# Two-layer mixture-of-experts block with a delta-net block behind it: expert weights in tiles of 256 rows, later modulation blocks, entry loads in pairs

## The chip, the core and the metric

The program runs on one core of a Trainium2 chip. The core has a matrix engine (TensorE, PE in the profile; PEld is its weight load), a vector engine (DVE), an activation engine (ACT), GpSimd (POOL), a sync engine (SP) that here issues nearly all transfers, and 16 DMA engines between HBM and the on-chip memory (SBUF, 128 partitions; PSUM for sums of matmuls). The metric is the device time of one execution in microseconds (us); lower is better. All data are fp32.

## What is computed

512 tokens of width 1024, and 256 context tokens, go through two layers, then through a second block (gated delta rule, dilated attention, a gated FFN). Of a layer this matters here:

```python
mods = silu(c) @ ada_w[l] + ada_b[l]          # 6 x 1024 numbers: shift, scale, gate of both halves
h = rms_norm(x, n1) * (1 + sc1) + sh1
p = split(h @ w_in)                           # 2304 columns: a_b a_c a_h b_v b_g c_q c_k c_v d_q d_k d_v
x = x + g1 * (concat(short_conv, conv31, window_attention, global_attention) @ w_out)
h2 = rms_norm(x, n2) * (1 + sc2) + sh2
gates, idx = top_k(softmax(h2 @ router).T, 64)     # 16 experts, each takes 64 tokens (32 of the context)
y = (silu(h2[idx] @ w_gate) * (h2[idx] @ w_up)) @ w_down     # three 1024 x 1024 matrices an expert
x = x + g2 * zeros.at[idx].add(y * gates)
```

Layer 0 does all of it for the context too (with modulations of its own), layer 1 only reads the context as keys and values. An expert's weights are 3 x 4 MB and are used once, so a layer streams 201 MB of them.

## The kernel before

One program, in this order: entry, layer 0 (mixing, w_out, routing, experts), layer 1 (the same), the second block. A tile scheduler puts each engine's instructions in order; an engine then runs its own list strictly in that order and waits at each instruction for the semaphores it needs. SP is such an engine: a transfer that must wait for a free buffer holds up all transfers behind it on SP. SP's transfers go round eight completion semaphores, and one waits until the transfer eight places ahead of it on SP has landed.

*Modulations.* `ada_gen` (L310) makes the 6144 numbers of a layer in 12 blocks of 512 columns. A block is four loads of 512 KB (`ada_load`, L196), matmuls (L318), an eviction (L323), transposes (L327) and two DVE steps. Having issued the matmuls of block b it loads pieces of block b+1 ahead, three or four of them (the `if` before L323). Layer 0's mixing runs blocks 4 to 11 of layer 0 and 0 to 7 of layer 1 beside the dense projections. Blocks 8 to 11 of layer 1 are run in layer 0's routing: one after the logits, the others between the steps of the top-k.

*The small pool.* All loads that are neither expert slots nor entry tiles use one pool of five `raw` tiles of 128 x 1024 (512 KB): modulation pieces, columns of w_in and w_out, and five expert tiles.

*Entry.* Small rows, x, the modulation blocks 0, 2, 1, 3 of layer 0 into a tile of their own (`ada0`), the context, and the first columns of w_in. The two tiles of c_q and of d_q take 64 columns from each of two places (`colload2`, L493; at the entry L272), which is 256 bytes a row. Then `norm1_first` (L390 to L398) makes h, split into a high and a low part (`hh`, `hl`), for all eight k.

*Dense projections.* `dense` (L427) goes over units of 128 columns. A unit's 512 KB are split by ACT (L442, `wh`) and POOL (L443, `wl`), and three products each (hh wh, hl wh, hh wl) over eight k are summed in PSUM (L473 for x, L475 for the context). Attention (L553 to L584) and the 31-tap convolution run between.

*Routing.* Logits (L974), softmax, eight rounds of max, index and replace on DVE (L1146 to L1149) for the top 64. The normalized tokens go to DRAM as `hd` (L1132), and each expert's tokens are gathered from it (L1209), transposed (L1221), and get shift and scale on eviction into `xt` (L1225 for x, L1228 for the context). In layer 0, `sumx` and `sumc` in DRAM are zeroed here (L1138, 3 MB): most experts add their output to them by an indirect transfer (L1300), the last are summed by matmuls with one-hot matrices.

*Experts.* Order of the work: gate of e, down of e-1, up of e. Each is eight tiles of 128 rows (`run_gu`, `down`, with `prod` L1237 in layer 1, L1243 and L1248 in layer 0). `wload` (L1044 to L1055) loads tiles in the order of use, one for each one used, into slots: A (18 or 20, tiles `rawA`), W (the five `raw`), B (2 or 8, `rawB`): 25 tiles in layer 0, 33 in layer 1. silu (L1273) and product (L1281) give `sa`, which is transposed (L1290, L1295) to `hT` for down. At the end of layer 0, `sums_load` brings back sumx and sumc, and `sums_add` (L1317 to L1321) transposes and adds them: the context's in the up of expert 15, x's in its down.

```python
slots = ["A"] * nA + ["W"] * 5 + ["B"] * nB
...
    SY.dma_start(r, W[w][l, e, 128 * u:128 * u + 128, :])
```

## Time and profile before

| | us |
|---|---|
| median of 3 runs (2655.12 to 2670.03) | 2669.66 |
| the profiled execution | 2663.15 |
| its span | 2660.6 |
| PE busy in the span | 2472.6 (93%) |
| mean granted clock of PE | 0.974 |

The profiled execution is 2.55 us longer than its span, and 6.5 us under the median. A stretch of the span is named by its start in us: entry 0 to 75, layer 0's mixing and w_out to 456, its routing to 501, its experts to 1056, layer 1's mixing and w_out to 1361, its routing to 1388, its experts to 1867, and the second block to 2660. "Busy" of PE counts a matmul from start to modelled end, so that a PE that waits a little for each weight tile can still read as busy all the time; there the DMA share (1 is all 16 engines busy) and the bytes tell which of the two sets the pace.

### The profile page before, as it was taken

The page shows a single profiled execution, that of the slowest core. Times are in us where ns is not written, and L with a number is a line of the kernel's source. Part 1 is how long each engine was busy: PE and PEld are TensorE (multiplying, and loading weights), DVE is VectorE, ACT ScalarE, POOL GpSimd, SP SyncE. Part 2 cuts the span into 40 slices and gives each one's busy share as a digit, 9 for nine tenths or more (in the row PEclk, how much of TensorE's full clock was granted, in tenths as well). Part 3 has the DMA queues.
Part 4 walks back from the last instruction along what each step waited for, and adds up shares of the span by engine and source line. Part 5 has one row for each costly group of instructions (what it writes and reads, how often), then busy time and mean ns, then how long its engine had stood idle before and what let it go on. Part 6 is the DMA issues. An engine that isn't in the chain of part 4 may idle for free.

```text
span 2660.6 us, 41308 instructions
## 1 busy us (share of the span) xinstructions
PE 2472.6 (93%) x16415; PEld 1498.3 (56%) x16415; DVE 1091.2 (41%) x2371; ACT 870.0 (33%) x1769; POOL 637.3 (24%) x552
## 2 busy tenths in 40 slices
PE   6999999799999999799979989898899999999998
PEld 3776777344444333677743212132578787888876
DVE  4488853311111114689641201021674555444411
ACT  4534362211111111465532111110552435434322
POOL 3423112011111100633220000000433323444443
PEclk9999999899999999799989999999899999999999
DMA  8455455999999998221279999999321102333321
GB/s 284 136 163 141 148 191 195 320 385 387 387 386 385 388 389 296 61 60 48 84 285 391 394 400 400 399 404 408 108 64 27 38 25 72 95 95 96 98 84 63
DMA packets 324758, 584.08 MB, mean 220 GB/s; under 512 B 36864, under 2 KB 190007, under 8 KB 323927
## 3 DMA queue, kind: packets, MB, share of 16 engines
q1 hardware_dynamic: 311943, 555.16, 57.6%
q0 software_dynamic: 12480, 26.23, 4.1%
q8 instruction: 129, 2.11, 0.3%
q14 instruction: 62, 0.51, 0.1%
q10 hardware_dynamic: 144, 0.08, 0.0%
HBM read 556.74 MB, written 18.87 MB: 216 GB/s over the span
## 4 chain that ended last, share of the span: by engine, by line
PE 65%; DMA 18%; DVE 9%; issue 3%; POOL 2%; ACT 1%; SPq 1%; ACTq 0%; DVEq 0%; POOLq 0%
PE px L473 20%; PE ax L1243 4%; DMA rawA<-in_w_down_dram 4%; PE yx L1243 3%; PE ux L1243 3%; PE g L473 2%; DMA rawA<-in_w_up_dram 2%; PE y L584 2%; PE px L475 2%; DMA rawA<-in_w_gate_dram 2%; PE s L553 2%; PE ux L1237 2%; PE pt L565 2%; PE ac L1248 2%; PE ax L1237 2%
## 5 line engine op out<-in xcount | busy, mean ns | idle before, releaser
L443 POOL TENSOR_TENSOR wl<-raw,wh 128x512 fp32r<-128x512 f32 (+1 forms) x312 | 408.7, 1313 | 968.0 <-ACT wh L442 908.2
L442 ACT ACTIVATE wh<-raw 128x512 fp32r<-128x512 f32 (+1 forms) x312 | 193.7, 625 | 440.5 <-PE px L473 207.7
L473 PE MATMUL px<-hh,wh 128*128 128x512 f32 x768 | 314.2, 410 | 6.4 <-DVE xT L1401 1.8
L473 PE MATMUL px<-hh,wl 128*128 128x512 f32 x768 | 311.8, 406 | 6.5 <-POOL wl L443 6.5
L473 PE MATMUL px<-hl,wh 128*128 128x512 f32 x768 | 313.7, 409 | 4.1 <-DVE hl L1019 1.9
L1225 ACT ACTIVATE xt<-tr,mod,a 128x64 f32<-128x64 f32 x256 | 87.0, 405 | 297.6 <-PE tr L1221 287.3
L473 PEld LDWEIGHTS px<-hh,wh 128*128 128x128 f32 x768 | 147.8, 193 | 40.9 <-issue 6.1
L473 PEld LDWEIGHTS px<-hh,wl 128*128 128x128 f32 x768 | 147.9, 193 | 39.5 <-POOL wl L443 7.2
L473 PEld LDWEIGHTS px<-hl,wh 128*128 128x128 f32 x768 | 148.2, 193 | 37.8 <-issue 3.8
L1369 DVE SCALAR_TENSOR_TENSOR Yx<-yx,gcol,Yx 64x512 fp32r<-64x512 f32 x36 | 27.0, 750 | 266.9 <-ACT Yx L1368 266.9
L1209 POOL DMA_INDIRECT xg<-hd,gidx x32 | 29.7, 928 | 432.2 <-PE tr L1221 399.0
L785 DVE SCALAR_TENSOR_TENSOR yT<-ub,cols,yT 128x512 f32<-128x512 f32 (+1 forms) x180 | 126.3, 717 | 0.6
L1243 PE MATMUL ax<-rawA,xt 128*32 128x512 f32 x856 | 117.2, 596 | 1.9 <-DMA rawA<-in_w_gate_dram 1.9
L1273 ACT ACTIVATE sa<-ax 128x512 f32<-128x512 f32 x32 | 19.1, 597 | 287.8 <-PE ax L1243 182.7
L1300 POOL DMA_INDIRECT sumx<-ys,place x14 | 22.0, 1571 | 376.7 <-ACT ys L1347 376.7
L1243 PE MATMUL ux<-rawA,xt 128*32 128x512 f32 x800 | 106.1, 594 | 0.9 <-DMA rawA<-in_w_up_dram 0.9
L1237 PE MATMUL ux<-rawA,xt 128*64 128x512 f32 x328 | 87.5, 611 | 8.3 <-DMA rawA<-in_w_up_dram 8.2
L1237 PE MATMUL yx<-rawA,hT 128*64 128x512 f32 x316 | 80.7, 610 | 12.6 <-DMA rawA<-in_w_down_dram 11.8
L565 PE MATMUL pt<-tab,P 128*128 128x128 f32 x448 | 83.7, 288 | 7.0 <-DVE PT L571 4.3
L1368 ACT ACTIVATE Yx<-yx,gcol 64x512 fp32r<-64x512 f32 x36 | 24.6, 682 | 191.1 <-PE yx L1237 139.3
L1228 DVE TENSOR_SCALAR xt<-tr,a,mod 128x32 f32<-128x32 f32 x128 | 39.1, 310 | 114.7 <-ACT xt L1225 114.2
L1237 PE MATMUL ax<-rawA,xt 128*64 128x512 f32 x316 | 77.4, 612 | 8.1 <-DMA rawA<-in_w_gate_dram 7.5
(593 smaller groups left out, 4887.5 us busy)
## 6 DMA issues: line engine op xcount, KB each, us to landing
rawA<-in_w_gate_dram SPq DMA_DIRECT2D x186, 512.0 KB
rawA<-in_w_up_dram SPq DMA_DIRECT2D x182, 512.0 KB
rawA<-in_w_down_dram SPq DMA_DIRECT2D x151, 512.0 KB
raw<-in_ada_w_dram SPq DMA_DIRECT2D x80, 512.0 KB
raw<-in_w_down_dram SPq DMA_DIRECT2D x74, 512.0 KB
raw<-in_w_gate_dram SPq DMA_DIRECT2D x62, 512.0 KB
raw<-in_w_in_dram SPq DMA_DIRECT2D x56, 512.0 KB
raw<-in_w_up_dram SPq DMA_DIRECT2D x55, 512.0 KB
```

Of the source, the lines that this page charges most:

```text
L442: A.activation(wh[:, :n], raw[i][:, a:a + n], AF.Copy)
L443: G.tensor_tensor(wl[:, :n], raw[i][:, a:a + n], wh[:, :n].bitcast(F32), op=OP.subtract)
L473: T.matmul(px, lhsT=w[:, k % 4, :], rhs=h[:, k0 + k, 0:512], start=st, stop=sp_)
L475: T.matmul(pc, lhsT=w[:, k % 4, :], rhs=h[:, k0 + k, 512:nt], start=st, stop=sp_)
L553: T.matmul(s[:, :w], lhsT=q, rhs=k, start=(a == 0), stop=(a == len(mm) - 1))
L565: T.transpose(pt[:, (t - a) * 128:(t - a + 1) * 128], P[:, t * 128:(t + 1) * 128], ident)
L584: T.matmul(y[64 * g:64 * g + 64, bi * 128:(bi + 1) * 128], lhsT=vs[g][t], rhs=PTs[i, g][t // 4][:, (t % 4) * 128:(t % 4 + 1) * 128], start ...
L785: V.scalar_tensor_tensor(acc[:, j, o:o + n], src, w, acc[:, j, o:o + n], op0=OP.mult, op1=OP.add)
L1225: A.activation(xt[:, kk, 0:64], p[:, k * NX:k * NX + 64], AF.Identity, bias=M[l][:, 24 + kk, 0:1], scale=a2[:, kk, 0:1])
L1237: T.matmul(px[64 * g:64 * g + 64, :], lhsT=lx(u), rhs=w[:, 512 * hf:512 * hf + 512], start=first, stop=last)
L1243: T.matmul(px[32 * g:32 * g + 32, :], lhsT=lx(u)[:, 32 * (g % 2):32 * (g % 2) + 32], rhs=w[:, 512 * hf:512 * hf + 512], start=first, stop= ...
L1248: T.matmul(pc[32 * g:32 * g + 32, :], lhsT=lc(u), rhs=w[:, 256 * q:256 * q + 256], start=first, stop=last)
```

## The change

*Expert weights.* A tile is now 256 rows: row 2p+i of it lies in partition p, half i, so that a partition reads 8 KB in one piece (`[128, 2, 1024]`, 1 MB, one transfer). A slots are nA/2 and B slots nB/2 such tiles. W is two pairs of `raw` tiles, each loaded by two transfers of 512 KB. That makes 12 pairs (24 tiles) in layer 0 and 16 pairs in layer 1. `wload(u % 2)` loads a pair for every second tile used.

Since a k step now holds every second row, the columns of `hd` and of `sa` are stored in the new order by the writes that make them (`pairs`, and the eviction into `ht`), and shift and scale are permuted into `shsc` by 8 small matmuls and two copies in the routing.

*Modulations.* Blocks 8 to 11 of layer 1 leave layer 0's routing and run in layer 1's mixing. The rule that loads pieces of the next block ahead stays as it was for block 7: three pieces of block (1, 8) are still loaded near the end of layer 0's mixing, into three `raw` tiles, and are now used only in layer 1's mixing.

*Entry.* x first, then blocks 0 and 2, the context, c_k's columns, blocks 1 and 3, c_q's columns, and the small rows behind them on SP. Blocks 1 and 3 are worked after the first half of the first dense unit, and `norm1_first` is cut into k 0 to 3 ahead of it and k 4 to 7 behind. The two tiles of c_q (and of d_q) come as two loads of 512 rows x 256 columns (`pair_load`, 1 KB a row) that serve both units.

*The rest.* The zeroing of sumx and sumc moves to the start of layer 0's mixing. `dense` in layer 1 gets the same limit on loads ahead as in layer 0 (`ahead=4`). The context's sums are loaded one expert earlier and added in the up of expert 14, those of x in the up and the down of expert 15, two of eight pieces at a time.

```diff
+    for t in range(1, 4):
+        x_load(t)
+    ada_load(0, 0, ada0[0])
+    ada_load(0, 2, ada0[2])
+    for t in range(2):
+        SY.dma_start(cin[:, t, :], I["ctx"][0, t * 128:(t + 1) * 128, :])
+    pre0 = {0: raw_tile().rearrange("p (k c) -> p k c", k=8)}
+    SY.dma_start(pre0[0], I["w_in"][0, :, 1536:1664].rearrange("(k p) c -> p k c", p=128))
+    ada_load(0, 1, ada0[1])
+    ada_load(0, 3, ada0[3])
+
+    def pair_load(src, c0):
+
+        ts = [raw_tile(), raw_tile()]
+        for i, t in enumerate(ts):
+            SY.dma_start(t.rearrange("p (k c) -> p k c", k=4),
+                         src[512 * i:512 * i + 512, c0:c0 + 256].rearrange("(k p) c -> p k c", p=128))
+        return ts
+
+    pre0[1] = pre0[2] = pair_load(I["w_in"][0], 1280)
...
             if 3 < b < 11 or (l == 1 and b != 7 and b < 11):
-                ada_load(l, b + 1, hfs=range(4 if l == 1 and b > 7 else 3))
+                ada_load(l, b + 1, hfs=range(3))
...
+                    a1 = cst.tile([128, 8, 2], F32)
+                    norm1_first(range(4), a1)
+                    gd = dense(units, hh, hl, dw, psp, pre=pre0, ahead=4)
+                    next(gd)
+                    drain(ada_gen(0, (1, 3), sqp, psp))
+                    norm1_first(range(4, 8), a1)
+                    entry.close()
...
-                ga = iter(())
                 if has:
                     def ada_rest():
                         yield from ada_gen(0, range(4, 12), sqp, psp)
                         yield from ada_gen(1, range(0, 8), sqp, psp)
                     ga = ada_rest()
-
-                gd = dense(u_c + u_b + u_d + u_a, hh, hl, dw, psp, pre=pre0 if has else {}, ahead=4 if has else None)
+                else:
+                    ga = ada_gen(1, range(8, 12), sqp, psp)
+
+                if not has:
...
+                    zz = sqp.tile([128, 512], F32, name="sq")
+                    G.memset(zz, 0.0)
+                    for acc_, n in zip(accs, (8, 4)):
+                        SY.dma_start(acc_.rearrange("(p a) c -> p (a c)", p=128).rearrange("p (b c) -> p b c", c=512),
+                                     zz[:, None, :].to_broadcast([128, n, 512]))
...
-            units = [(w, e, u) for w, e in seq for u in range(8)]
+            units = [(w, e, u) for w, e in seq for u in range(4)]
             W = {"g": I["w_gate"], "u": I["w_up"], "d": I["w_down"]}
             wt = {}
             nload = [0]
-            slots = ["A"] * nA + ["W"] * 5 + ["B"] * nB
+            slots = ["A"] * (nA // 2) + ["W"] * 2 + ["B"] * (nB // 2)
             rwpB = [None]
 
             def wload(n):
+
                 for _ in range(n):
                     i = nload[0]
                     if i >= len(units):
                         return
                     w, e, u = units[i]
                     k = slots[i % len(slots)]
+                    src = W[w][l, e, 256 * u:256 * u + 256, :].rearrange("(p i) c -> p i c", i=2)
                     if k == "W":
-                        r = raw_tile()
-                    elif k == "A":
-                        r = rwpA.tile([128, 1024], F32, name="rawA", bufs=nA)
+                        r = [raw_tile(), raw_tile()]
+                        for j in range(2):
+                            SY.dma_start(r[j], src[:, j, :])
                     else:
-                        r = rwpB[0].tile([128, 1024], F32, name="rawB", bufs=nB)
-                    SY.dma_start(r, W[w][l, e, 128 * u:128 * u + 128, :])
-                    wt[w, e, u] = r
+                        if k == "A":
+                            t = rwpA.tile([128, 2, 1024], F32, name="rawA", bufs=nA // 2)
+                        else:
+                            t = rwpB[0].tile([128, 2, 1024], F32, name="rawB", bufs=nB // 2)
+                        SY.dma_start(t, src)
+                        r = [t[:, 0, :], t[:, 1, :]]
+                    for j in range(2):
+                        wt[w, e, 2 * u + j] = r[j]
                     nload[0] += 1
 
-            wload(nA if has else nA + 5)
-            if has:
-                ada_load(1, 8)
+            wload(nA // 2 + 2)
...
-                    ga = ada_gen(1, range(8, 12), mp, Psum(ps, {"yx": 1}, {"misc": "yx"})) if has else iter(())
...
-                    for _ in steps(ga, 2):
-                        pass
-                    wload(6 if l else 0)
+                    wload(3 if l else 0)
+
...
+                    pc = psp.tile([128, 512], F32, name="misc")
+                    mview = M[l][:, 24:32, :].rearrange("p (a h) s -> p h a s", h=2), \
+                        a2.rearrange("p (a h) s -> p h a s", h=2)
+                    for q, mv in enumerate(mview):
+                        for h in range(2):
+                            for i in range(2):
+                                c = 16 * q + 8 * i
+                                T.matmul(pc[64 * h:64 * h + 64, c:c + 8], lhsT=ident[:, i::2], rhs=mv[:, h],
+                                         start=True, stop=True)
+                    for q in range(2):
+                        V.tensor_copy(shsc[:, q].rearrange("p (a i) s -> p i a s", i=2),
+                                      pc[:, 16 * q:16 * q + 16].rearrange("p (i a s) -> p i a s", i=2, s=2))
 
...
-                            A.activation(ht[:, hf * 512:(hf + 1) * 512], p, AF.Copy, scale=r[:, t:t + 1])
+                            A.activation(ht[:, hf * 512:(hf + 1) * 512].rearrange("t (a i p) -> t a i p", a=2, i=2),
+                                         p.rearrange("t (a p i) -> t a i p", a=2, i=2), AF.Copy, scale=r[:, t:t + 1])
                         SY.dma_start(hd[t * 128:(t + 1) * 128, :], ht)
-                    wload(nB - (6 if l else 0))
-                    if has:
-                        zz = sqp.tile([128, 1024], F32, name="ht", bufs=4)
-                        G.memset(zz, 0.0)
-                        for acc_, n in zip(accs, (512, 256)):
-                            SY.dma_start(acc_.rearrange("(p a) c -> p (a c)", p=128).rearrange("p (b c) -> p b c", c=1024),
-                                         zz[:, None, :].to_broadcast([128, n // 128, 1024]))
+                    wload(nB // 2 - (3 if l else 0))
...
+                def pairs(x, ordered):
+
+                    if ordered:
+                        return x.rearrange("t (a i p) -> t a i p", i=2, p=128)
+                    return x.rearrange("t (a p i) -> t a i p", i=2, p=128)
 
                 def act(e):
                     ax, ac = acc.pop(("g", e))
                     sa = sp.tile([128, NX * 8], F32, name="sa")
-                    A.activation(sa[:, 0:512], ax, AF.Silu)
+                    A.activation(pairs(sa[:, 0:512], 1), pairs(ax, 0), AF.Silu)
                     if has:
...
```

Three places show how the instructions stand. In these rows a name with a number is one tile; without, it stands for any tile of that name, and xN is a run of N alike.

First, SP's list at the entry, before, from the first modulation block (`ada` is its tile) on:

```order
L196 DMA ada_89<-in_ada_w_dram 128x2x512 x2
L229 DMA rows<-in_conv_qkv_dram 48x128
L229 DMA rows<-in_ffn_conv_dram 66x128
L196 DMA ada_89<-in_ada_w_dram 128x2x512 x6
L265 DMA cin<-in_ctx_dram 128x1024 x2
L196 DMA ada_89<-in_ada_w_dram 128x2x512 x4
L269 DMA raw<-in_w_in_dram 128x8x128
L272 DMA raw<-in_w_in_dram 128x8x64 x2
L196 DMA ada_89<-in_ada_w_dram 128x2x512 x4
```

and now, from the last loads of x on:

```order
L239 DMA xin<-in_x_dram 128x1024 x3
L199 DMA ada_96<-in_ada_w_dram 128x2x512 x4
L199 DMA ada_97<-in_ada_w_dram 128x2x512 x4
L252 DMA cin<-in_ctx_dram 128x1024 x2
L254 DMA raw<-in_w_in_dram 128x8x128
L199 DMA ada_94<-in_ada_w_dram 128x2x512 x4
L199 DMA ada_95<-in_ada_w_dram 128x2x512 x4
L262 DMA raw<-in_w_in_dram 128x4x256 x2
L232 DMA raw<-in_q_norm_g_dram 2x64 x2
```

The rows of 64 columns (L272) and the small rows no longer stand among the modulation blocks; c_k's columns stand ahead of blocks 1 and 3 (`ada_94`, `ada_95`), and c_q's pair behind them.

Second, SP's list in layer 0's experts, before, from the down of expert 0 to the gate of expert 2:

```order
L1055 DMA rawA<-in_w_down_dram 128x1024 x6
L1055 DMA rawA<-in_w_up_dram 128x1024 x8
L1055 DMA rawA<-in_w_gate_dram 128x1024 x3
L1055 DMA raw<-in_w_gate_dram 128x1024 x5
L1055 DMA rawB<-in_w_down_dram 128x1024 x2
L1055 DMA rawA<-in_w_down_dram 128x1024 x6
L1055 DMA rawA<-in_w_up_dram 128x1024 x8
```

and now, from the last up tiles of expert 1 on. `raw_4415` and `raw_4416` are the third pair of expert 1's gate, `raw_4934` and `raw_4935` the second pair of expert 2's:

```order
L1088 DMA rawA_4874<-in_w_up_dram 128x2048
L1088 DMA rawA_4892<-in_w_up_dram 128x2048
L1082 DMA raw_4415<-in_w_gate_dram 128x1024
L1082 DMA raw_4416<-in_w_gate_dram 128x1024
L1088 DMA rawA_4916<-in_w_gate_dram 128x2048
L1082 DMA raw_4934<-in_w_gate_dram 128x1024
L1082 DMA raw_4935<-in_w_gate_dram 128x1024
L1088 DMA rawB_4985<-in_w_gate_dram 128x2048
```

Before, five `raw` tiles follow one another and the tiles after them. Now the third pair of a gate stands behind the up tiles of its expert, which are used later than it, and only two `raw` tiles are free: SP issues `raw_4415` when PE has used `raw_4411`, the half of the second pair that lay in the same place, and `raw_4934` when PE has used `raw_4415`.

Third, PE's list at that place in layer 0's experts, before (the gate of expert 1):

```order
L1243 MATMUL ax_5019<-raw_4621,xt_4948 32x512 x4
L1248 MATMUL ac_5020<-raw_4621,xt_4948 32x256 x4
L1243 MATMUL ax_5019<-raw_4623,xt_4948 32x512 x4
L1248 MATMUL ac_5020<-raw_4623,xt_4948 32x256 x4
L1290 MATMUL tr_5062<-tab_70,sa_4903 128x128 x4
L1295 MATMUL tr_5068<-tab_70,sa_4903 128x128 x2
L1243 MATMUL ax_5019<-raw_4752,xt_4948 32x512 x4
L1248 MATMUL ac_5020<-raw_4752,xt_4948 32x256 x4
L1243 MATMUL ax_5019<-raw_4754,xt_4948 32x512 x4
L1248 MATMUL ac_5020<-raw_4754,xt_4948 32x256 x4
```

and now:

```order
L1276 MATMUL ax_4898<-rawA_4409,xt_4831 32x512 x4
L1281 MATMUL ac_4899<-rawA_4409,xt_4831 32x256 x4
L1276 MATMUL ax_4898<-raw_4411,xt_4831 32x512 x4
L1281 MATMUL ac_4899<-raw_4411,xt_4831 32x256 x4
L1276 MATMUL ax_4898<-raw_4412,xt_4831 32x512 x4
L1281 MATMUL ac_4899<-raw_4412,xt_4831 32x256 x4
L1329 MATMUL tr_4939<-tab_72,sa_4790 128x128 x4
L1334 MATMUL tr_4945<-tab_72,sa_4790 128x128 x2
L1276 MATMUL ux_5070<-rawA_4811,xt_4831 32x512
L1276 MATMUL yx_4990<-rawA_4734,hT_4938 32x512
L1276 MATMUL ax_4898<-raw_4415,xt_4831 32x512 x4
L1281 MATMUL ac_4899<-raw_4415,xt_4831 32x256 x4
L1276 MATMUL yx_4990<-rawA_4734,hT_4938 32x512
L1276 MATMUL ax_4898<-raw_4416,xt_4831 32x512 x4
```

Now a few transposes (L1329, L1334) and single matmuls of up and down stand between the second pair (`raw_4411`, `raw_4412`) and the third (`raw_4415`, `raw_4416`), and everything else of the expert stands behind the third.

## Rows read from the trace of the kernel before

**Rows 1.** The page, part 2: busy tenths in 40 slices of 66.5 us each.
```profile
PE   6999999799999999799979989898899999999998
...
DMA  8455455999999998221279999999321102333321
```

**Rows 2.** Stretches: busy us of PE, PEld, DVE, ACT, POOL; clock, DMA share, GB/s.
```profile
75.00:400.00 325.00, 312.08 (x2055) 235.44 (x2055) 234.07 (x599) 156.38 (x358) 87.91 (x78) 0.96 0.51 157
520.00:880.00 360.00, 360.00 (x4363) 149.36 (x4359) 54.08 (x142) 48.57 (x123) 41.61 (x31) 1.00 1.03 387
880.00:1056.00 176.00, 170.59 (x1905) 63.99 (x1901) 40.65 (x112) 24.89 (x58) 14.77 (x14) 1.00 0.98 367
1090.00:1300.00 210.00, 194.34 (x1150) 152.73 (x1151) 168.47 (x376) 116.80 (x263) 85.35 (x72) 0.95 0.23 58
1388.00:1867.00 479.00, 431.06 (x1832) 126.68 (x1830) 72.28 (x106) 71.35 (x175) 12.38 (x14) 1.00 1.02 395
1867.00:2660.00 793.00, 760.78 (x3824) 606.41 (x3824) 374.90 (x654) 335.78 (x587) 312.73 (x243) 0.99 0.25 71
```

**Rows 3.** Chain of waits, 20 to 80 us: start us, length us, what.
```profile
25.87 4.32 SPq L272
30.23 3.60 SPq L272
...
36.47 7.75 DMA ada<-in_ada_w_dram
...
47.21 0.82 ACT hh L396
...
63.79 0.51 PE px L475 x2
```

**Rows 4.** Chain of waits, layer 0's routing and the end of its experts.
```profile
454.56 1.79 PE s L974 x13
...
461.58 4.11 DMA raw<-in_ada_w_dram
...
479.51 15.32 DMA raw<-in_ada_w_dram
...
500.86 0.99 PE ax L1243 x8
...
506.88 5.90 DMA raw<-in_ada_w_dram
...
1055.17 1.04 PE yx L1243 x8
```

**Rows 5.** Chain of waits, layer 1's routing.
```profile
1360.70 0.44 PE s L974
...
1387.80 4.54 PE ax L1237 x13
```

**Rows 6.** DMA queue 1, 600:700, 880:952, 1500:1800 us: packets, MB, share.
```profile
q1 hardware_dynamic: 9928, 36.15, 92.4%
...
q1 hardware_dynamic: 6833, 24.89, 88.7%
...
q1 hardware_dynamic: 32375, 117.88, 99.9%
```

**Rows 7.** Stretches as above: a reload in 8 KB rows, a store, the weights.
```profile
378.00:382.00 4.00, 4.00 (x35) 3.75 (x34) 4.00 (x6) 1.31 (x4) 2.74 (x2) 1.00 1.00 420
43.00:48.00 5.00, 2.01 (x10) 0.56 (x8) 0.76 (x6) 1.39 (x3) 0.00 (x0) 1.00 1.03 431
1785.00:1815.00 30.00, 27.00 (x118) 6.89 (x114) 2.88 (x4) 4.54 (x11) 0.00 (x0) 1.00 1.03 409
```

**Rows 8.** PE by line, 75:400, then 985:1056 us: count, busy us, mean ns.
```profile
L318 PE MATMUL misc<-raw,s 128*32 128x512 f32 x256 | 36.2, 599 | 0.2 <-DVE sq L723 0.2
...
L327 PE MATMUL misc<-tab,sq 128*128 128x128 f32 x64 | 10.1, 275 | 0.0
...
L1317 PE MATMUL tr<-tab,rb 128*128 128x128 f32 x44 | 9.2, 297 | 1.6 <-DMA rb<-sumx 1.6
```

More of the change, by code (lines that the diff above doesn't have):

```diff
@@ L172, in main_kernel @@
     xcT = xp.tile([128, 8, 256], F32)
[L173 removed]
+    dxp = pool(ctx, "dx", space=DRAM)
+    dx = dxp.tile([128, 8 * 768], F32)
+    accs = dxp.tile([1024, 512], F32, name="sumx"), dxp.tile([1024, 256], F32, name="sumc")
     stA = cst.tile([128, 768], F32)
@@ L332, in ada_gen, with rows_to_cols @@
             yield
+    def rows_to_cols(psp, name, g, n):
+        p = psp.tile([128, 512], F32, name=name)
+        T.transpose(p[:, :n], rows[0:n, g, :], ident[0:n, 0:n])
+        V.tensor_copy(cols[:, g, 0:n], p[:, :n])
     es_l0 = ExitStack()
@@ L379, in main_kernel, with norm1_first @@
             drain(ga)
-            for g in (0, 2, 3):
-                rows_to_cols(g, RO["n", g])
-            V.tensor_scalar(nsink, sinkb, -1.0, None, op0=OP.mult)
-        entry.close()
-        def norm1_first(sqp):
-            a1 = sqp.tile([128, 8, 2], F32, name="a1")
-            for k in range(8):
+        entry2.close()
+        def norm1_first(ks, a1):
+            for k in ks:
                 if k % 4 == 0:
@@ L429, in load @@
                     raw[i] = pre[i]
+                elif i < len(units) and len(units[i]) == 6 and units[i][5]:
+                    raw[i] = raw[i - 1]
+                elif i < len(units) and len(units[i]) == 6:
+                    raw[i] = units[i][0]()
                 elif i < len(units):
@@ L938, in layer @@
                     ga = ada_rest()
-                gd = dense(u_c + u_b + u_d + u_a, hh, hl, dw, psp, pre=pre0 if has else {}, ahead=4 if has else None)
+                else:
+                    ga = ada_gen(1, range(8, 12), sqp, psp)
+                if not has:
+                    gd = dense(units, hh, hl, dw, psp, ahead=4)
                 at, cv = att_gen(), conv31()
                 w1, w2, w3 = (28, 28, 64) if has else (18, 18, 44)
-                run_all((dense_part(gd, 12), 12))
-                run_all((dense_part(gd, 12), 12), (steps(at, w1), w1), (steps(ga, 8), 8))
+                g1 = 8 if has else 2
+                if has:
+                    for _ in range(2):
+                        next(gd)
+                    for g in (0, 2, 3):
+                        rows_to_cols(psp, "misc", g, RO["n", g])
+                    V.tensor_scalar(nsink, sinkb, -1.0, None, op0=OP.mult)
+                    zz = sqp.tile([128, 512], F32, name="sq")
[3 more added lines that the diff above has]
+                                     zz[:, None, :].to_broadcast([128, n, 512]))
+                run_all((dense_part(gd, 9 if has else 12), 12))
+                run_all((dense_part(gd, 12), 12), (steps(at, w1), w1), (steps(ga, g1), g1))
                 c1 = 16 if has else 8
-                run_all((dense_part(gd, 12), 12), (steps(at, w2), w2), (steps(ga, 8), 8), (steps(cv, c1), c1))
-                run_all((gd, 18), (at, w3), (ga, 16), (cv, (42 if has else 21) - c1))
+                run_all((dense_part(gd, 12), 12), (steps(at, w2), w2), (steps(ga, g1), g1), (steps(cv, c1), c1))
+                run_all((gd, 18), (at, w3), (ga, 16 if has else 4), (cv, (42 if has else 21) - c1))
                 for k in (4, 5, 6, 7, 2, 3, 0, 1):
@@ L1080, in experts @@
                 gidx = mp.tile([128, 16], I32)
+                shsc = mp.tile([128, 2, 8, 2], F32)
                 iota = mp.tile([128, 512], F32)
@@ L1181, in experts @@
                         V.tensor_copy(gidx[0:64, :], tok[0:64, 0:16])
-                wload(5 if has else 0)
                 if has:
@@ L1280, in mul @@
                     sa = acc["s", e]
-                    V.tensor_tensor(sa[:, 0:512], ux, sa[:, 0:512], op=OP.mult)
-                    if has:
-                        V.tensor_tensor(sa[:, 512:768], uc, sa[:, 512:768], op=OP.mult)
+                    for u_, o, n in ((ux, 0, 512), (uc, 512, 256))[:2 if has else 1]:
+                        c = sa[:, o:o + n]
+                        V.tensor_tensor(pairs(c, 1), pairs(u_, 0), pairs(c, 1), op=OP.mult)
                 def hpose(e):
@@ L1340, in down @@
                         prod(px, pc, e, u, r, lx, lc, u == 0, u == 7)
-                        wload(1)
-                        if has and e == 15:
-                            sums_add(u)
+                        wload(u % 2)
+                        if has and e == 15 and u % 2:
+                            sums_add(4 + u // 2)
                     if has and e < 14:
@@ L1455, in experts @@
                         if has and e == 15:
-                            run_gu("u", e, [], sums_add)
+                            run_gu("u", e, [], lambda u: sums_add(u // 2))
+                        elif has and e == 14:
+                            run_gu("u", e, mid, lambda u: sums_add(8 + u // 2))
                         else:
@@ L1460, in experts @@
                         gather(e + 2)
-                        if has and e in (13, 14):
-                            for t in ((4, 5), range(4))[e - 13]:
+                        if has and e in (12, 14):
+                            for t in ((4, 5), range(4))[e // 2 - 6]:
                                 sums_load(t)
```

104 lines of the change are left out of this document (40 added, 64 removed).

## The prediction, written before the changed kernel was run

> **What bounds the kernel now.** I read the page's slices first [rows 1]. PE is near full over most of the span and the DMA engines are full only twice, in slices 8 to 16 and 21 to 28: the two expert stages. The table by stretch gives each stage its limit [rows 2]. Layer 0's mixing has PE busy for 312.08 of 325 us at a DMA share of 0.51, layer 1's for 194.34 of 210 at 0.23: PE-bound, with 13 and 15.7 us of idle time. Layer 0's experts have both full from 520 to 880. One expert there is 24 weight tiles of 16 matmuls and 14 transposes, 398 instructions, so 360 us x 398 / 4363 = 32.8 us per expert is PE's pace. DMA's pace comes from the queue totals [rows 6]: an expert is 24 x 0.524 = 12.58 MB; 36.15 MB in 100 us makes one in 34.8 us, 24.89 MB in 72 us one in 36.4, on average 35.6. So PE used weights faster than they came, by some 2.8 us an expert, and lived on the 25 tiles loaded ahead (25 x 1.28 us = 32 us, ten to twelve experts' worth); from about 880 on DMA sets the pace. Layer 1's experts need 117.88 MB in 300 us, 32.0 us each, with PE far below that: DMA-bound. The second block is PE-bound and untouched. The chains show what the routings and the entry wait for [rows 3 to 5].
>
> **The change, part by part.** The sum is made against the profiled execution, 2663.15 us (span 2660.6 and 2.55 around it). It lies 6.5 us under the median of the three runs; I leave that gap alone.
>
> *Entry: -12 us (-16 to -8).* The last modulation block lands at 36.47 + 7.75 = 44.2 us, and ahead of it SP spent 4.32 + 3.60 = 7.9 us on the 256-byte rows of L272 [rows 3]. They are now replaced and stand behind, as do the small rows, so block 3 lands about 8 us earlier. From there to the first products took 63.79 - 47.21 = 16.6 us for the eight k of h. Now four k are made before block 3 is needed: if all of that half shows, 8.3 us more. I take half of it, since POOL has the same splits to do.
>
> *Layer 0's mixing: 0 (-3 to +3).* The same matmuls in a PE-bound stage; the zeroing's 3 MB fall where the DMA share is 0.51 [rows 2]. If that cover fails, 3 MB at 409 GB/s are 8 us of DMA, of which PE would see a part.
>
> *Layer 0's routing and experts, taken together: -4 us (-39 to +34).* Before, the last logits end at 456.4, and the first expert matmul comes at 500.9, held up by modulation pieces: waits of 4.11 and 15.32 us, and one of 5.90 inside the first gate [rows 4]. These go. Without them layer 1 takes from 1361.1 to 1387.8, 26.7 us [rows 5]; layer 0 has six token tiles in place of four, so I take 487, between 456.4 + 26.7 = 483 and the 494.9 at which the last piece landed. That alone is 14 us, and the first gate loses its 5.90 too.
>
> Against this stands a loss. Three `raw` tiles hold block (1, 8) through all of layer 0's experts, and the two pairs of slot W share the other two. SP's rows in the section on the change show it: the third pair of each gate is loaded only when PE has used the second, and next on PE, but for some transposes and single matmuls, stands the third. So once an expert PE waits for a load that has just been issued, and all later tiles queue behind it on SP. The trace of before has no such wait in its experts. Its bounds: nothing (the half pair is issued 1.4 us early and short work covers the rest), or 4.11 us, the wait for a late modulation piece [rows 4]. I take the middle, 2.1: the pace by latency is then 32.8 + 2.1 = 34.9 us. DMA gives the same number. A pair in 8 KB rows should run like the 8 KB reload at 420 GB/s, against 409 for the weights in 4 KB rows [rows 7]: 1.049 MB take 2.497 us in place of 2.564. Ten of an expert's twelve pairs gain, 0.67 us, and 35.6 - 0.67 = 34.9. (The bounds: no gain at 409; 431, the rate of the store, 1.31 us.) With the load of every expert tied to the use of the pair before it, work loaded ahead can no longer be drawn down over ten experts, so this pace holds from the start.
>
> The stage, then: 487; 20 tiles to the end of expert 1's second pair, 20 x 32.8 / 24 = 27.3; fourteen experts at 34.9, 488.6; a tail of 28 tiles, 38.3, with one wait of 2.1 and the 9.2 us of transposes of `sums_add` [rows 8]. It ends at 1052.5, against 1055.17 + 1.04 = 1056.2 [rows 4]: -3.7. The better overlap of `sums_add` is in the tail. The ends: 483, 32.8 and no wait give 1017; 494.9, 36.9 and a wait of 4.1 give 1090.
>
> *Layer 1's mixing: +8 (0 to +17).* Four modulation blocks come in. Sixteen blocks took 36.2 + 10.1 us of PE in layer 0's mixing [rows 8], 2.9 each, so 11.6 us; the 15.7 us of idle time [rows 2] can take part of that, and I give it a third. Until block 8 is used, the dense loads have only two `raw` tiles: up to 5 us more.
>
> *Layer 1's routing: +1 (0 to +3).* The 8 small matmuls and two copies for `shsc` stand beside a top-k on DVE that takes longer than they do; if that cover fails, they cost what some tens of short PE instructions cost.
>
> *Layer 1's experts: -10 (-21 to 0).* Here all five `raw` tiles are free, and 14 of 16 pairs have 8 KB rows: 10.5 pairs an expert, 0.70 us (0 to 1.38). (384 - 33) / 24 = 14.6 experts' tiles are loaded inside the stage: 10 us of a DMA-bound stage [rows 6, 7]. What is late next is DMA still: PE has room.
>
> A rule that promises far more: the Trainium skill, "DMA: Bandwidth & Descriptors", section "Anatomy of one DMA", fits a transfer's time as 2.0 us plus its bytes at 436 GB/s, and so asks for 1 MiB and more; by it 1 MB in one transfer would be 2 us shorter than in two. The trace disagrees for a full queue: 24 tiles of 0.5 MB came in 32.0 us, 1.33 us each, so no fixed cost shows there, and the sum has none.
>
> Sum: -12 + 0 - 4 + 8 + 1 - 10 = -17, from 2663 to 2646. About 1%, 27 us, is what a measurement of this kernel can tell from no change; this is less.
>
> **Rivals.**
> *A. The wait on the third pair is long.* If the just-issued load stands behind others as the modulation piece of 5.90 us did [rows 4], an expert takes 38.7 us and the tail 3.8 more: 487 + 27.3 + 541.8 + 53.4 = 1109.5, +53 on the stage, and the whole is 2663 - 12 + 53 + 8 + 1 - 10 = 2703, slower. It decides from 36.1 us an expert on (a wait of 3.3), where the stage's loss eats the other -13. For it: the DMA share of 1.03 [rows 2] means there is a queue to stand behind. Against: SP is blocked before that load, so the queue has had time to run dry.
> *B. No wait shows.* PE keeps 32.8: 487 + 27.3 + 459.2 + 47.5 = 1021, -35 on the stage, 2615. For it: the half pair's head start and a load ahead of nine pairs. Against: 32.8 is below DMA's 34.9, and 24 tiles ahead can't be drawn down.
> *C. Longer rows don't help.* At 409 GB/s as before: 14 x 0.67 + 10 = 19 us less gain, 2665, no change. Against: two other transfers with long rows ran at 420 and 431 [rows 7], though one is four microseconds long and the other a store.
> *D. A fixed cost per transfer, as in the rule above.* With any part of it, layer 1's stage would shrink by tens of us: below 2620. Nothing in rows 6 speaks for it.
>
> **How the numbers follow.** Forecast 0.50, B 0.22, C 0.14, A 0.13, D 0.01. Faster by over 1% is most of B, D, and the quarter of the forecast in which the entry or layer 1 gives more: 0.20 + 0.01 + 0.15 = 0.36. Slower by over 1% is most of A and a little of C: 0.12. Within 1%: 0.52. The range leaves out half of B and half of A: 2612 to 2685. The forecast's own is 2630 to 2662.
>
> **What would show it.** In the changed kernel's profile: block 3's load landing near 36 us; no wait for `raw<-in_ada_w` in layer 0's routing and the first expert matmul near 475 (487 less the entry's 12); gate phases of layer 0 some 2 us longer than the up phases, with waits for `raw<-in_w_gate` once an expert, and experts 34.9 us apart from the second on; 420 GB/s in place of 409 in quiet stretches of layer 1's experts, which take about 469 us. The prediction is wrong if layer 0's experts run at 32.8 to the end (B) or beyond 36 (A), or if the quiet rate stays at 409 (C).

## The result and the profile after

The changed kernel takes 2681.62 us (median of 5 runs, 2679.11 to 2688.46), the kernel before 2664.08 beside it: a ratio of 1.0073, 95% interval 1.0057 to 1.0089. It is slower by 0.7%, which is clear of the noise; forecast were 2646 us and a gain. The profiled execution is the longest of the five, 2688.46, so its stages add up to 26 us more than before, where the medians differ by 17.5.

The stages, read off PE's rows (the last logits, the first and the last expert matmul of a layer):

| stage, us | before | after | difference | forecast |
|---|---|---|---|---|
| start to the last logits of layer 0 | 456.8 | 456.2 | -0.6 | -12 |
| to the first expert matmul | 44.0 | 30.2 | -13.8 | -14 |
| layer 0's experts | 555.4 | 592.0 | +36.6 | +10 |
| to the last logits of layer 1 | 305.0 | 312.7 | +7.7 | +8 |
| to the first expert matmul | 26.7 | 28.5 | +1.8 | +1 |
| layer 1's experts | 478.9 | 473.3 | -5.6 | -10 |
| the rest | 794.0 | 793.9 | -0.1 | 0 |

(The forecast named layer 0's routing and experts together, -4; 487 and 1052.5 in its working give the two rows.) One stage carries the loss. The page's tenths, as in [rows 1], hardly tell the two kernels apart: in the first expert stage, slices 9 to 15, PE and DMA read 9 here as there, since 9 stands for all from 90% up. The table by stretch is finer (columns as in [rows 2]):

```profile
520.00:880.00 360.00, 344.15 (x3979) 147.20 (x3982) 49.59 (x130) 43.64 (x110) 40.77 (x30) 1.00 0.95 353
880.00:1078.00 198.00, 184.53 (x2068) 79.02 (x2064) 40.03 (x112) 25.35 (x60) 16.30 (x16) 0.97 0.91 343
1420.00:1893.00 473.00, 418.91 (x1832) 136.58 (x1828) 72.09 (x106) 70.72 (x174) 12.11 (x14) 0.98 1.01 400
```

From 520 to 880 us PE ran 3979 instructions, where it ran 4363: 360 x 398 / 3979 = 36.0 us an expert in place of 32.8. And the DMA engines are not the reason, since their share fell as well, from 1.03 to 0.95 and, further on, from 0.98 to 0.91. Both wait. In layer 1's experts the rate has gone up, from 395 to 400 GB/s. The waits in layer 0's experts, first of PE and then of SP's queue (us in total, times, the longest):

```profile
PE ax L1276 <- DMA raw<-in_w_gate_dram: 21.5, 17, 3.5
```

```profile
SPq L1082 <- PE ac L1281: 183.8, 49, 14.7
SPq L1082 <- DMA raw<-in_w_gate_dram: 93.3, 23, 14.1
```

Line 1082 loads slot W's pairs. PE waits 21.5 us for them. Before, its largest wait for weights of this stage was

```profile
PE ax L1243 <- DMA rawA<-in_w_gate_dram: 1.9, 2, 1.1
```

SP stands for 183.8 us at line 1082 until PE has used the tile that lay in the place, and for 93.3 more until an earlier transfer has landed, with everything else queued behind. (The earlier transfer is the third pair itself, where the next gate's second pair waits; late in the stage it is also the second pair, where the third waits.) This is the place that the section on the change shows. The starts of the up and gate matmuls give the pace (duration min, median, max in ns; first and last start):

```profile
L1276 PE MATMUL ux<-rawA,xt x1024: 592/592/617, 497.9 to 1060.2; 128*32 128x512 f32 x171
...
L1276 PE MATMUL ax<-raw,xt x480: 592/592/1063, 511.7 to 1036.9; 128*32 128x512 f32 x160
```

Fifteen experts lie between the first up tile of the first and of the last expert. The last up phase starts 11.7 us before its last matmul, so an expert takes (1060.2 - 11.7 - 497.9) / 15 = 36.7 us. By the same count the kernel before has 33.9, with its slower experts at the end.

PE's waits of 21.5 us, 1.3 an expert, are less than half of the loss. The rest hides in PE's busy time. At one expert PE's list ran so (start and length in us; in brackets the wait before):

```profile
625.91 1.05 PE L1276 MATMUL ux<-rawA,xt 128*32 128x512 f32 x2
...
628.46 1.06 PE L1276 MATMUL ax<-raw,xt 128*32 128x512 f32 x8 [0.22 <-DMA raw<-in_w_gate_dram]
...
632.39 1.94 PE L1276 MATMUL ax<-raw,xt 128*32 128x512 f32 x8 [2.43 <-DMA raw<-in_w_gate_dram]
```

The scheduler has put twelve up and down matmuls ahead of the third pair here (4 to 36 at other experts). They start in uneven groups and take from 625.91 to 628.46, where the sixteen matmuls of a weight tile, which start four at a time, take 1.3 us. Summed from each start of a matmul to the next, between the second and the thirteenth gate, an expert takes 3.6 us more than in e1 below: some 2.2 lie in the gate, in waits and in matmuls at a lower clock, and some 1.4 in up and down.

### The profile page after: what moved, and what is told of

Read it like the earlier page. It is cut to its first block, busy times and chain, and to the rows that moved or that the text cites. A ratio compares the mean times of both kernels' runs of the same rounds, so it can differ in the third digit from the quotient of the medians.

```text
span 2686.7 us, 40579 instructions
## 1 busy us (share of the span) xinstructions
PE 2475.8 (92%) x16447; PEld 1531.1 (57%) x16447; DVE 1096.4 (41%) x2375; ACT 869.0 (32%) x1769; POOL 632.4 (24%) x545
## 4 chain that ended last, share of the span: by engine, by line
PE 38%; DMA 13%; DVE 5%; ACT 1%; issue 1%; POOL 0%; ACTq 0%; DVEq 0%; SPq 0%; POOLq 0%
PE px L486 17%; DMA rawA<-in_w_down_dram 4%; DMA rawA<-in_w_gate_dram 3%; PE g L486 2%; DMA rawB<-in_w_down_dram 2%; PE pt L486 2%; PE s L560 2%; PE ux L1270 2%; PE s L486 1%; PE y L591 1%; PE ax L1270 1%; DMA rawB<-in_w_up_dram 1%; PE misc L486 1%; DMA raw<-in_w_up_dram 1%; PE yx L1270 1%; PE pt L572 1%
## 5 line engine op out<-in xcount | busy, mean ns | idle before, releaser
L1258 ACT ACTIVATE xt<-tr,shsc 128x64 f32<-128x64 f32 x256 | 85.8, 405 | 276.4 <-PE tr L1254 270.1
L1276 PE MATMUL yx<-rawA,hT 128*32 128x512 f32 x976 | 165.4, 594 | 4.1 <-DVE hT L1330 4.1
L1276 PE MATMUL ux<-rawA,xt 128*32 128x512 f32 x1024 | 156.8, 594 | 0.0
L1281 PE MATMUL yc<-rawA,hT 128*32 128x256 f32 x976 | 120.4, 379 | 0.0
L1281 PE MATMUL uc<-rawA,xt 128*32 128x256 f32 x1024 | 101.6, 379 | 0.0
L1390 DVE TENSOR_SCALAR yt<-yc,gcol 128x256 f32<-128x256 f32 x12 | 5.8, 484 | 219.1 <-PE yc L1281 219.1
L1276 PE MATMUL ax<-raw,xt 128*32 128x512 f32 x480 | 71.5, 622 | 21.6 <-DMA raw<-in_w_gate_dram 21.5
L1270 PE MATMUL yx<-rawA,hT 128*64 128x512 f32 x288 | 70.9, 626 | 21.1 <-DMA rawA<-in_w_down_dram 21.0
```

The source lines that it names most:

```text
L1258: A.activation(xt[:, kk, 0:64], p[:, k * NX:k * NX + 64], AF.Identity, bias=shsc[:, 0, kk, 0:1], scale=shsc[:, 1, kk, 0:1])
L1270: T.matmul(px[64 * g:64 * g + 64, :], lhsT=lx(u), rhs=w[:, 512 * hf:512 * hf + 512], start=first, stop=last)
L1276: T.matmul(px[32 * g:32 * g + 32, :], lhsT=lx(u)[:, 32 * (g % 2):32 * (g % 2) + 32], rhs=w[:, 512 * hf:512 * hf + 512], start=first, stop= ...
L1281: T.matmul(pc[32 * g:32 * g + 32, :], lhsT=lc(u), rhs=w[:, 256 * q:256 * q + 256], start=first, stop=last)
```

## The experiments

Each has the kernel before beside it on the same chip. Stages are of one profiled execution each, in us; the time is the median.

| kernel | time | ratio to before (95%) | to logits | routing 0 | experts 0 | mixing 1 | experts 1 |
|---|---|---|---|---|---|---|---|
| changed | 2681.62 | 1.0073 (1.0057 to 1.0089) | 456.2 | 30.2 | 592.0 | 312.7 | 473.3 |
| e1_free_raws | 2631.63 | 0.9898 (0.9874 to 0.9922) | 451.0 | 30.2 | 540.5 | 311.3 | 471.8 |
| e2_zeros_late | 2665.37 | 1.0023 (1.0010 to 1.0035) | 446.6 | 30.0 | 579.0 | 312.7 | 473.2 |
| e3_both | 2627.28 | 0.9878 (0.9858 to 0.9898) | 443.1 | 30.0 | 541.5 | 313.4 | 472.1 |
| e4_one_w_pair | 2629.75 | 0.9882 (0.9861 to 0.9903) | 453.9 | 30.2 | 542.5 | 313.7 | 472.3 |
| e5_4k_rows | 2638.37 | 0.9912 (0.9895 to 0.9928) | 448.1 | 31.3 | 543.8 | 311.1 | 478.6 |
| e6_ada_routing | 2633.06 | 0.9893 (0.9876 to 0.9909) | 447.5 | 35.9 | 547.6 | 303.6 | 472.5 |
| e7_q_64 | 2631.95 | 0.9886 (0.9867 to 0.9905) | 449.7 | 30.4 | 541.2 | 312.9 | 471.5 |
| e8_w_on_pool | 2764.24 | 1.0400 (1.0360 to 1.0440) | 448.6 | 30.0 | 675.6 | 312.4 | 472.3 |

**e1_free_raws: the three raw tiles.**

```diff
-            if 3 < b < 11 or (l == 1 and b != 7 and b < 11):
+            if b < 11 and (b > 3 if l == 0 else b != 7):
                 ada_load(l, b + 1, hfs=range(3))
```

Expected: 

> The changed kernel, but three pieces of block (1, 8) are no longer loaded near the end of layer 0's mixing: all five raw tiles are free in layer 0's experts, so the third pair of a gate no longer waits for the second. Theory (the tied third pair makes layer 0's experts 36.7 us apart): they go back to 32.8 us at first and to DMA's pace of about 34.9 later, the stage from the first gate to the last down shrinks from 592 us to between 535 and 555, and the time falls by 37 to 57 us, to 2625 to 2645. Rival (the stage is slow because 1 MB transfers and 24 tiles ahead feed PE worse): at most 10 us faster. Block (1, 8) is now loaded late in layer 1's mixing: up to 5 us there.

Measured: 50 us less than the changed kernel, the stage 540.5 in place of 592.0. The same stretch as above:

```profile
520.00:880.00 360.00, 359.92 (x4364) 149.09 (x4357) 54.51 (x143) 47.97 (x121) 44.84 (x33) 1.00 1.03 388
```

PE's pace is back at the 32.8 us of [rows 2] (4364 instructions), with the DMA engines full; over the fifteen experts it is 33.6. No up or down matmul stands ahead of a third pair any more. What is left of waiting for weights in the stage is this row, and it is for a down tile:

```profile
PE yx L1276 <- DMA rawA<-in_w_down_dram: 2.8, 3, 1.7
```

The rival is out: with 1 MB transfers and 24 tiles ahead PE is fed as before. Late loads of block (1, 8) cost nothing that shows, 311.3 against 312.7 in layer 1's mixing.

**e4_one_w_pair: the tie without the tiles.**

```diff
-            slots = ["A"] * (nA // 2) + ["W"] * 2 + ["B"] * (nB // 2)
+            slots = ["A"] * (nA // 2) + ["W"] * (1 if has else 2) + ["B"] * (nB // 2)
...
-            wload(nA // 2 + 2)
+            wload(nA // 2 + (1 if has else 2))
```

Expected: 

> The changed kernel with the three raw tiles still held, but slot W has one pair in place of two in layer 0: 11 pairs instead of 12, and no pair that waits for the one just ahead of it. Theory (the tie is the cause, not the number of tiles): the wait for raw<-in_w_gate goes, and the stage shrinks by 30 to 50 us, 2632 to 2652. Rival (too few tiles ahead is the cause): no faster than the changed kernel, or slower by up to 10 us.

Measured: 52 us less than the changed kernel, with two tiles fewer and the three raw tiles held as they were. The stretch, and what remains of PE's wait for `raw<-in_w_gate` (21.5 us in the changed kernel):

```profile
520.00:880.00 360.00, 359.24 (x4351) 148.67 (x4347) 54.59 (x143) 47.20 (x119) 44.92 (x33) 1.00 1.02 388
```

```profile
PE ax L1276 <- DMA raw<-in_w_gate_dram: 0.5, 1, 0.5
```

So it is not how many tiles are loaded ahead, but that two pairs, used one right after the other, shared one place. (Both edits rid PE of the wait and its list of the early matmuls; no run takes these two apart.)

**e8_w_on_pool: what the wait is made of.**

```diff
-                            SY.dma_start(r[j], src[:, j, :])
+                            (G if has else SY).dma_start(r[j], src[:, j, :])
```

Expected: 

> The changed kernel with the three raw tiles still held, but in layer 0 the loads of slot W are issued by POOL, so that a third pair that waits for the second no longer holds up SP and what is queued behind. If the price of the tie is that SP stands still and the DMA engines run dry: the stage comes near e1's 540 us, 2630 to 2645. If it is the third pair's own latency, behind what is already in the queue: PE goes on waiting for raw<-in_w_gate, and the time stays within 15 us of the changed kernel, 2667 to 2690.

Measured: worse than either account; 83 us slower than the changed kernel. SP no longer stands at these loads, and PE waits for them far longer:

```profile
PE ax L1276 <- DMA raw<-in_w_gate_dram: 77.4, 19, 8.8
```

The row of these loads, over 520 to 1100 us, gives the time from issue to landing, which the profile has for POOL's transfers (KB each, median us):

```profile
raw<-in_w_gate_dram POOLq DMA_DIRECT2D x53, 512.0 KB, 7.7
```

The third pair is issued when PE has used the second, and PE needs it almost at once. The 7.7 us are the median over both pairs of slot W; from the issue of a third pair's first tile to PE's first matmul on it pass 7.0 to 11.1 us. PE waits 77.4 us in place of 21.5: 56 of the 83. Much of the rest goes with the lower clock after these waits, 0.94 on average over the stretch below; a matmul `ax<-raw` takes 764 ns on average, in the changed kernel 622. So the pair's own latency is the price, as the second account had it, though far more of it than that account expected. Two things probably add to the wait here. SP runs on and fills the queue with the tiles behind. The microsecond before the issue of a third pair, in the changed kernel and then here (columns as in [rows 2], DMA share next to last):

```profile
696.60:697.60 1.00, 1.00 (x20) 0.41 (x16) 0.00 (x0) 0.00 (x0) 0.00 (x0) 1.00 0.39 143
```

```profile
675.00:676.00 1.00, 1.00 (x17) 0.39 (x12) 0.00 (x0) 0.00 (x0) 0.00 (x0) 1.00 1.08 336
```

In the changed kernel the share is 0.0 to 0.8 from the fourth pair on. The three pairs before that met a full queue, and PE used them 4.7, 8.0 and 7.1 us after SP's issue, two of them near POOL's times. And in PE's list here only four matmuls stand ahead of the third pair, so PE reaches it sooner. No run separates these two from a cost of POOL's own. The DMA engines are less busy over the stage too, since PE, waiting, frees tiles later:

```profile
520.00:1100.00 580.00, 509.16 (x5522) 203.64 (x5518) 75.90 (x202) 64.67 (x162) 84.57 (x95) 0.94 0.89 321
```

The Trainium skill, "DMA: Bandwidth & Descriptors", section "Issuing engines are not separate DMA queues", has it that transfers started by different engines end up on the same 16 DMA engines and interleave. The 7.7 us agree with it: another issuer gave the urgent pair no way past the others.

**e2_zeros_late and e3_both: the entry's gain.** In the changed kernel the first products start at 34.4 us instead of 48.1, and by 120 us most of that lead is gone. SP's queue from 44 to 70 us:

```profile
SPq L969 <- POOL sq L967: 15.1, 1, 15.1
```

Line 969 zeroes sumx. It waits for a memset on POOL that stands behind POOL's splits, and the columns of w_in stand behind it on SP: they are issued at 63.5 us, in e3_both at 46.9.

```diff
-                    zz = sqp.tile([128, 512], F32, name="sq")
-                    G.memset(zz, 0.0)
-                    for acc_, n in zip(accs, (8, 4)):
...
                 run_all((dense_part(gd, 12), 12), (steps(at, w2), w2), (steps(ga, g1), g1), (steps(cv, c1), c1))
+                if has:
+                    zz = sqp.tile([128, 512], F32, name="sq")
+                    G.memset(zz, 0.0)
+                    for acc_, n in zip(accs, (8, 4)):
...
                 run_all((gd, 18), (at, w3), (ga, 16 if has else 4), (cv, (42 if has else 21) - c1))
```

Expected of the first: 

> The changed kernel, but sumx and sumc are zeroed late in layer 0's mixing. Theory (SP waits 15.1 us at the zeroing for POOL, and the columns of w_in stand behind it and its 3 MB, which eats the entry's 10 us): the first w_in columns after the entry land some 15 us earlier, and w_out ends 8 to 10 us earlier, 2672 to 2674. Rival (what the entry gains is lost in the attention's and the convolution's own chains): 0 to 3 us.

Expected of the second, which has e1's edit too: 

> Both edits together, block (1, 8) not loaded ahead and the zeroing late. If both theories hold, 45 to 67 us faster than the changed kernel, 2615 to 2637, and 27 to 49 faster than the kernel before. If neither holds, within 13 us of the changed kernel.

Measured: by the ratios 0.5% or 13 us less than the changed kernel, and 0.2% or 5 us less on top of e1 (there the intervals overlap). The stretch from 70 to 100 us, of the changed kernel and of e3_both:

```profile
70.00:100.00 30.00, 22.92 (x108) 17.27 (x107) 8.55 (x21) 9.74 (x19) 18.09 (x20) 0.83 0.72 171
```

```profile
70.00:100.00 30.00, 26.89 (x165) 21.77 (x164) 14.16 (x35) 14.09 (x32) 20.00 (x22) 1.00 0.54 147
```

165 instructions of PE in place of 108, with its clock at full rate in place of 0.83. How much of it stays at the last logits is less sure. Four kernels with the early zeroing (changed, e1, e4, e8) reach them at 456.2, 451.0, 453.9 and 448.6, four with the late one (e2, e3, e5, e6) at 446.6, 443.1, 448.1 and 447.5: on average 452.4 and 446.3, so 6 us, with a spread of 5 to 8 us among kernels nearly alike up to there. The rival, 0 to 3 us, is unlikely, and the 8 to 10 of the theory were too much. The two edits don't add up either: of e2's 13 us some lie in a shorter experts' stage (579.0 against 592.0), which e1's edit takes away anyway.

**e5_4k_rows: the length of the rows.**

```diff
-                        SY.dma_start(t, src)
                         r = [t[:, 0, :], t[:, 1, :]]
+                        for j in range(2):
+                            SY.dma_start(r[j], src[:, j, :])
```

Expected: 

> The kernel with both edits (e3_both), but each pair of slots A and B comes by two transfers of 512 KB in 4 KB rows at a pitch of 8 KB, as slot W's pairs do: the same bytes into the same places. Theory (a quiet queue moves 8 KB rows at 419 GB/s and 4 KB rows at 409): layer 1's experts 5 to 10 us longer, layer 0's 3 to 7, 2635 to 2644. Rival (the row's size is worth nothing; layer 1's gain has another source): within 3 us of e3_both, 2624 to 2630. Second rival (a fixed cost for each transfer): tens of us slower.

Measured: 11 us more than e3_both, 6.5 of it in layer 1's experts and 2.3 in layer 0's, the rest in stages that the edit hardly touches. A quiet stretch of layer 1's experts in e3_both, then in this kernel (the last column is GB/s):

```profile
1790.00:1820.00 30.00, 26.75 (x118) 8.49 (x120) 6.36 (x10) 1.96 (x3) 0.00 (x0) 1.00 1.01 417
```

```profile
1740.00:1770.00 30.00, 29.30 (x135) 10.21 (x135) 6.73 (x11) 4.43 (x11) 0.00 (x0) 1.00 1.03 409
```

417 against 409. The theory holds with its smallest numbers (6.5 where it had 5 to 10, 2.3 where it had 3 to 7), and twice the number of transfers cost nothing beyond the rate: the second rival is out.

**e6_ada_routing: what the moved blocks are worth.** The zeroing is late here too; of the edit, the core:

```diff
-                    ga = ada_gen(1, range(8, 12), sqp, psp)
+                    ga = iter(())
...
+                    ga = ada_gen(1, range(8, 12), mp, Psum(ps, {"yx": 1}, {"misc": "yx"})) if has else iter(())
...
+                        if i in (2, 4, 6):
+                            for _ in steps(ga, 2):
+                                pass
```

Expected: 

> The changed kernel with the zeroing late, and blocks 8 to 11 of layer 1 back in layer 0's routing as in the kernel before; the pieces of block (1, 8) are then used up before the experts, so the raw tiles are free there too. Theory (the move pays 14 us in the routing and costs 8 in layer 1's mixing, and the tie of the third pair is gone here as well): layer 0's routing 14 to 20 us longer than in e3_both, layer 1's mixing 7 to 9 shorter, 2633 to 2641. Rival (the move gains nothing by itself): within 3 us of e3_both.

Measured: 6 us more than e3_both; the two intervals of the ratio overlap by half, so the sign is likely and the size is not sure. By stages, the routing is 5.9 us longer and the experts 6.1 (a piece of the last block is still waited for inside the first gate), the mixing 9.8 shorter. PE's wait for modulation pieces from 448 to 520 us, in the kernel before and then here:

```profile
PE yx L318 <- DMA raw<-in_ada_w_dram: 16.2, 4, 14.0
```

```profile
PE yx L326 <- DMA raw<-in_ada_w_dram: 4.2, 2, 2.4
```

The zeroing's 3 MB are no longer in that stretch, which probably is why. The routing's 5.9 us are far less than the theory's 14 to 20, so the blocks' move by itself is worth little. And the tie is gone here too (547.6 with the blocks in it), as it must be if the held tiles made it.

**e7_q_64: 64 columns at a time.**

```diff
-                            units.append((partial(pair_load, w_in, c0[n]), ev, nt, 0, 8, j))
+                            units.append((colload2(w_in, c0[n] + 64 * j, c0[n] + 128 + 64 * j), ev, nt))
```

Expected: 

> The kernel with both edits (e3_both), but the columns of c_q and d_q come 64 at a time again (256 bytes a row), in the new order of the entry. Theory (the 256-byte rows held up SP for 7.9 us at the entry): w_out ends 4 to 10 us later than in e3_both, layer 1's mixing up to 3 us longer, 2632 to 2640. Rival (the order of the loads gave the entry's gain, not the pairs): within 3 us.

Measured: 2631.95, with 2627.19 to 2633.70 against e3_both's 2624.17 to 2628.71. The intervals of the ratio overlap by most of their width, and the 6.6 us at the last logits are within the spread named above. Inconclusive: up to 5 us, or nothing. With 449.7 against 456.8 before, most of the entry's gain is there without the pairs; whether it comes from the new order of the loads or from cutting `norm1_first` in two was not tested.

## Why the prediction was wrong, step by step

*Layer 0's experts: the step that failed.* The prediction found the place and the mechanism, and rival A, "the wait on the third pair is long", is what happened: it was to decide from 36.1 us an expert on, and over the fifteen experts the pace is 36.7. What failed is the size of the wait, the sentence "I take the middle, 2.1", between nothing and the 4.11 us of a late modulation piece [rows 4]. Measured, the third pair costs 36.0 - 32.8 = 3.2 us an expert from 520 to 880 us, and 36.7 - 33.6 = 3.1 over all fifteen, with e1 as the kernel without it. The 4.11 was PE's wait for another load, and no row had the time that counts here, from SP's issue to the landing. By the completion semaphores, the first tile of the pair lands 3.7 to 8.7 us after its issue and the second, issued 1.3 us later, 6.3 to 8.7. Against A stood that "the queue has had time to run dry". From the fourth pair on it had, nearly (0.39 above); but a pair that is issued only when PE is about to need it comes late all the same. And some 1.4 of the 3.6 us that an expert takes longer than in e1 stand in no term of the sum: the up and down matmuls that the scheduler puts ahead of the third pair.

The second half of the step misled as well: "DMA gives the same number", 34.9, looked like a confirmation. One 34.9 holds a guessed 2.1, and the other is a pace only while no tiles loaded ahead are left: e1 runs at 32.8 into its thirteenth expert. In the changed kernel the DMA share of 0.95 shows that neither number set the pace. Fourteen experts x 1.8 us (36.7 - 34.9) are 25 of the 26.5 us by which this row was missed (592.0 - 555.4 = 36.6, where 487 and 1052.5 make 10). With the tie gone the stage is 540.5 (e1) or 542.5 (e4), and with it 592.0, or 579.0 in e2: it cost 37 to 52 us, where the 592.0 is of the longest of five executions. Rival B, "no wait shows", was near in that case, 2615 us against e1's 2632. Against B stood that "24 tiles ahead can't be drawn down"; once each load is free of the pair before it, they are.

*Entry, -12, of which 0.6 was left at the last logits.* The first products came 13.7 us earlier, inside the range given, but in part by luck. The last modulation piece lands at 38.7 us in place of 44.2, so 5.5 us earlier and not 8. And "From there to the first products took 63.79 - 47.21" misreads its row: 63.79 is a later step of the chain, and before, the first products started at 48.1. Now they start at 34.4, ahead of blocks 1 and 3, so the 13.7 us came by another path than the one that was summed. The cost was put beside it and not in it: "the zeroing's 3 MB fall where the DMA share is 0.51", hidden, under layer 0's mixing at 0. Bytes were counted, and SP's list was not: the transfer waits 15.1 us for POOL, and the columns of w_in stand behind it. With the late zeroing the last logits come 456.8 - 446.3 = 10.5 us earlier than before on average of four kernels, so the term's size was near; with the early one 4.4.

*Layer 0's routing, -14: right*, 13.8. But not for the reason given alone, so in part by luck: in e6, with the blocks in the routing as before and the zeroing gone from it, the routing takes 35.9 in place of 44.0. The blocks' move gives 6 of the 14, other parts of the change, probably the zeroing's leaving, 8; no run took them apart.

*Layer 1's mixing, +8: right*, 7.7, with two sizes off in opposite ways. Four blocks took PE, over the stage (columns as [rows 8]),

```profile
L326 PE MATMUL misc<-raw,s 128*32 128x512 f32 x64 | 11.0, 601 | 0.2 <-DMA raw<-in_ada_w_dram 0.2
...
L335 PE MATMUL misc<-tab,sq 128*128 128x128 f32 x16 | 3.1, 316 | 0.0
```

14.1 us, more than the 11.6 worked out from layer 0; if the rest of the stage took what it took before, close to half of it went into time that had been idle, where a third was given. The up to 5 us for the lack of raw tiles did not show: e1, with all five free, has 311.3 against 312.7, though its later loads of block (1, 8) may hide a gain.

*Layer 1's routing, +1: right*, 1.8.

*Layer 1's experts, -10: the right mechanism, too large.* The term was 1.049 MB at 420 GB/s, from a stretch of four microseconds [rows 7]. The weights came at 417, so a pair gains 2.564 - 2.516 = 0.048 us; x 10.5 x 14.6 = 7. Measured 5.6, and 6.5 by e5. Rival C (no gain) and rival D (a cost per transfer, here in a full queue of SP) are both out by e5.

Together: the range (2612 to 2685) held the time, the direction was wrong, and one term did most of it, with the entry's as the second. A version that beats both kernels came out of it: e3_both, at 0.9878 (0.9858 to 0.9898) of the kernel before, two small edits away from the changed one.

## What to carry to other kernels

When a change keeps a buffer for longer, count what is left in its pool at every later user, and look for two users that now share one place back to back: there PE pays the time from issue to landing at each use, whatever is loaded ahead elsewhere, so look for rows that show that time before giving the wait a size. On an engine that issues transfers in order, ask of every transfer put among others not only how many bytes it moves but what it waits for, since all behind it wait too. And two limits that come to the same number (here a latency and a bandwidth, both 34.9) are no confirmation of each other when one of them holds a guess.

## What the runs showed of the hardware that was not expected

Moving urgent loads to another issuing engine did not make them earlier: a third pair's first tile was used 7.0 to 11.1 us after POOL's issue, where it landed 3.7 to 8.7 us after SP's in the changed kernel, and the kernel became 83 us slower. A queue that has run nearly dry does not make such a load quick: with a DMA share of 0.39 in the microsecond before the issue at 697.6 us, the pair's tiles landed 5.3 and 7.2 us after theirs.

Also, after some of its waits PE ran gate matmuls at half rate: the longest of `ax<-raw` is 1063 ns against a median of 592 in the changed kernel, where in e1 the longest of that group is 617; the granted clock over 880 to 1078 us was 0.97 against 1.00 for the same stage before [rows 2]. After the wait of 2.43 us that ends at 632.39 it was 0.50, the lower of its two levels, from 633 to 635 us. So a wait can cost PE somewhat more than its own length. In e8, with waits of up to 8.8 us, the clock was 0.94 over 580 us; how much of its loss that is was not measured.
